# Differential attention on one core: values in halves between the heads, two output sums ahead of the last head, raw tiles of 4 KB

## The chip, the core and the metric

The kernel runs on one core of one Trainium2 chip. The metric is the device time of one execution in microseconds (us), the median of several runs. Engines are named as in the profile: PE is TensorE's matmul, PEld its weight load, DVE VectorE, ACT ScalarE, POOL GpSimd, SP SyncE, which issues the DMAs here.

## What is computed

Two layers of a transformer trunk on 512 tokens of width 1024, in float32. Each layer is a feed-forward block, a token mixer, a cross-attention into 256 memory tokens and a second feed-forward block, each followed by a layer norm. The mixer of layer 0 is differential attention; the mixer of layer 1 pools. The change lies in differential attention alone:

```python
q, k, v = jnp.split(x @ w_qkv, 3, axis=-1)       # 8 heads; q, k: 2 maps of 64; v: 128 wide
q, k = rope(q, c5, s5), rope(k, c5, s5)
...
s = jnp.where(mask, q k^T * scale, min)           # for both maps of a head
p = jax.nn.softmax(s, axis=-1)
a = p[:, :, 0] - lam * p[:, :, 1]
o = a @ v                                         # per head
...
o = o * rsqrt(mean(o * o) + eps) * subln_g * (1 - lam_init)
return o.reshape(B, S, H * 2 * dk) @ w_o
```

## The kernel before

Every float32 matmul is made of three: each factor is split into a high and a low part, and `mm3` (line 219) issues high x high, high x low and low x high into the same sums, 24 matmuls for a column block of 512 over the depth of 1024. I call one such group of three a triple. Weights come from memory into a raw tile by one DMA on SP's queue, ACT casts the raw tile to its high part (`wh`), and DVE subtracts for the low part (`wl`). The tags `wh` and `wl` have five slots each in this stage, of 4 KB per partition; `raw` has two slots of 8 KB.

**The stage of attention** is woven from two streams (`weave`, line 228). The main stream, `da_main` (line 1251), is a generator of projections: after each triple it yields the time that the planner books for it, `3 * max(107, columns * 0.42)` ns: 645 for 512 columns and 323 for 256. The side stream, `da_side` (line 1278), is one head's chain of small steps after another. It yields a weight after each step, and the next step is emitted when main has booked weight x `GAP` = 900 ns more. A step that isn't allowed yet yields `WAIT`, and the credit is set to zero. Head h may start when main's clock is `LEAD` = 6000 ns past the time at which its key was finished. When main is exhausted, what is left of the side stream is emitted without anything between (`drain`, line 242).

The emitted order is the priority by which a list scheduler fills each engine's queue with the help of its own model of times: an operation that it thinks not ready can be passed by later ones, and on the chip every queue then runs strictly in the order laid down. So the last three score matmuls of head 7 stand behind some output sums that were emitted after them.

**Main** goes over pairs of heads. `da_values` (line 1113) loads the value weights of a pair (256 columns, 1 MB, one raw tile), splits them into two tiles of `wh` and `wl`, and computes the values of all 512 tokens in two blocks of 16 triples of 256 columns, two token tiles in each block; after a block the sums are split into a value tile `v` (four slots). `raw_heads` (line 279) loads the query or key weights of a pair, 512 KB for each head, and `cols_rope` (line 287) splits those of one head. Then for each head 8 triples of 512 columns for the query, the rotation `da_rope` (line 1129: shuffle and multiply on DVE, a multiply on POOL, an add on DVE) with a split, and the same for the key. Pairs 0 to 2 have their values ahead of their heads; pair 3 (`V_FIRST` = 6) behind them. At the end of main stand eight output sums over heads 0 to 3 (`to_tokens`, line 513: four triples of 512 columns and an add on DVE for each half and token tile, rows of `da_w_o` through `rows`, line 310, four at a time). So main's order is values 0, heads 0 and 1, values 1, heads 2 and 3, values 2, heads 4, 5, 6 and 7, values 3, sums.

**Side**, for each head: `da_scores` (line 1150), 24 matmuls into six PSUM banks, then for each of four row blocks and two maps a DVE operation that adds the mask and takes the maximum (L1174) and an exponential on ACT; then `STEPS` (line 46). A mix (`da_mix`, L1190 to L1192) combines the two maps on DVE and is queued behind the last mask; turn i (`da_turn`) transposes i + 1 blocks on TensorE and splits them on ACT and DVE; last turns out the head before (`da_turn_out`: four transposes, and a split into `oT`); out i (`da_out`) is i + 1 pairs of matmuls against the values. After out 1 and out 3 the sums are copied and added, and after out 3 a root on POOL and a scaling of `o` follow. A mix yields no weight. The weights `W` (line 39): 4.6 after the scores, (1.0, 1.0, 1.2, 1.5) for the turns, (0.8, 0.8, 1.2, 2.0) for the outs, 0.8 for the last head's scaling, 1.0 for last: 15.1 for a whole head.

Behind the weave `diff_attention` (line 1303) adds the second half of the output sums, over heads 4 to 7. Of the first two of these sums five triples (heads 4 to 6) are put ahead of the last head's transposes (`ready` = 3), and they use the two PSUM banks of the tag `mm`; their weights are split into tiles of `qk`, `low` and `p` that the heads have left.

Of the kernel before, what the change touches and what calls it, by code (L numbers as in the profile page):

```python
# [17 lines left out]
P = 128  # L18
D = 1024
S = 512  # L20
NT = S // P
KC = D // P
# [4 lines left out]
ALPHA = (2 * DEPTH) ** 0.25  # L27
EPS = 1e-5
DA_H = 8
# [5 lines left out]
BAND = P + 16  # L35


V_FIRST, LEAD, GAP = 6, 6000, 900
W = dict(
    scores=4.6,  # L40
    turn=(1.0, 1.0, 1.2, 1.5),
    out=(0.8, 0.8, 1.2, 2.0),
    scale=0.8,
# [66 lines left out]
def drain(units):  # L110
    for _ in units:
        pass
# [7 lines left out]
class Trunk:  # L120
# [65 lines left out]
    @contextmanager  # L186
    def stage_pools(self, w, raw, order):

        with ExitStack() as ctx:
            self.stage = {}  # L190
            for n in order:
                if n == "wh" == order[0]:
                    self.to_w(ctx)
                if n == "mem":
                    self.to_x(ctx)
                self.stage[n] = ctx.enter_context(self.pool(n))
            self.banks = {n: ctx.enter_context(self.pool(n, space=PSUM)) for n in ("px", "py", "yz")}
            self.w_bufs, self.raw_bufs, self.aux_turn = w, raw, 0
            yield

    def raw_tile(self, shape, tag="raw"):
# [26 lines left out]
    def weave(self, main, side, gap, lead=0):  # L228


        self.clock, credit, weight = 0, -lead, 1.0
        for ns in main:
            self.clock += ns
            credit += ns
            while credit >= gap * weight:
                credit -= gap * weight
                weight = next(side, WAIT)
                if weight is WAIT:
                    credit, weight = 0, 1.0
                weight = weight or 1.0  # L240
        self.clock = float("inf")
        drain(side)
# [33 lines left out]
        self.split_weights(w[0], w[1], raw[:, :, j * P : (j + 1) * P])  # L276
        return w

    def raw_heads(self, w, c0):

        raw = self.raw_tile((2, KC, P))
        for j in range(2):
            c = c0 + j * P
            self.nc.sync.dma_start(raw[:, j], w[:, c : c + P].rearrange("(k p) n -> p k n", p=P))
        return raw

    def cols_rope(self, raw, j, wait=False):

        nc = self.nc
        w = self.hl([P, 8, P])  # L290
        src = raw[:, j].rearrange("p k (m h q e) -> p (k m) q h e", m=2, h=2, q=2)
        hi, lo = (t.rearrange("p k (m q h e) -> p (k m) q h e", m=2, q=2, h=2) for t in w)
        nc.scalar.copy(hi, src)
        with self.tc.issue_after(self.turned[1].ins) if wait else nullcontext():
            for q in range(2):
                self.last_low = nc.vector.tensor_sub(
                    lo[:, :, q], src[:, :, q], hi[:, :, q].bitcast(F32)
                )
        return w
# [10 lines left out]
    def rows(self, w, k0, kn, c0, homes=None):  # L310


        got = []
        for k in range(0, kn, 4):
            n = min(4, kn - k)
            raw = self.raw_tile((4, S))
            r0 = (k0 + k) * P
            self.nc.sync.dma_start(
                raw[:, :n], w[r0 : r0 + n * P, c0 : c0 + S].rearrange("(k p) n -> p k n", p=P)
            )  # L320
            if homes:
                got += [home() for home in homes]
                for j, t in enumerate(got):
                    self.split(t[0], t[1], raw[:, j])
                continue
            for j in range(0, n, 2):
                t = self.hl([P, 2, S])
                self.split_weights(t[0], t[1], raw[:, j : j + 2])
                got += [(t[0][:, i], t[1][:, i]) for i in range(2)]
        return got  # L330
# [182 lines left out]
    def to_tokens(self, parts, w, k0, kn, first, last, scale, homes=(None, None), ready=None):  # L513

        nc = self.nc
        ws, sums = [None, None], []
        self.sum_begins, self.sum_ends = [], []
        ready = ready or kn
        for n, (half, t) in enumerate(LAST if last else sorted(LAST)):
            c = slice(half * S, (half + 1) * S)  # L520
            if t == 0:
                ws[half] = self.rows(w, k0, kn, half * S, homes[half])

            def some(ps, t, ks):
                o = slice(t * P, (t + 1) * P)
                for k in ks:
                    h = parts[k]
                    ns = self.mm3(ps, (h[0][:, o], h[1][:, o]), ws[half][k], k == 0, k == kn - 1, ready < kn)
                    if k == 0:
                        self.sum_begins.append(self.first_mm)  # L530
                    yield ns

            if n == 0 and ready < kn:
                out_turns = self.turns
                for tok in range(2):
                    sums.append(self.mm("ps"))
                    yield from some(sums[tok], tok, range(ready - tok))
                for turn in out_turns:
                    self.queue_behind(turn, self.last_mm)
                yield from some(sums[1], 1, (ready - 1,))  # L540
            if n < len(sums):
                ps = sums[n]
                yield from some(ps, t, range(ready, kn))
            else:
                ps = self.mm("ps")
                yield from some(ps, t, range(kn))
            self.sum_ends.append(self.last_mm)
            if last:
                self.summed(half, t, scale if first else 1.0, ps)
            else:  # L550
                X = self.X[t][:, c]
                nc.vector.scalar_tensor_tensor(
                    X, X, scale if first else 1.0, ps, ALU.mult, ALU.add
                )


    def ffn(self, layer, j, ln, beside=()):
# [552 lines left out]
        nc.vector.tensor_scalar(n, n, LAM_INIT, -1.0, ALU.add, ALU.mult)  # L1110
        return n

    def da_values(self, h, vs):

        raw = self.raw_cols(self.a["da_w_qkv"][0], 2 * D + h * P)
        ws = self.wide(raw)
        for t in range(0, NT, 2):
            ps = self.mm("v").rearrange("p (t n) -> p t n", t=2)
            for i in range(2):
                o = (t + i) * P  # L1120
                for k in range(KC):
                    yield self.mm3(ps[:, i], self.xs(k, o, o + P), ws[k], k == 0, k == KC - 1)
            self.turn_late()
            v = self.act("v", (P, 2, 2, 2, P))
            ps = ps.rearrange("p t (h n) -> p t h n", h=2)
            self.split(v[:, :, :, 0], v[:, :, :, 1], ps)
            vs += [v[:, i] for i in range(2)]

    def da_rope(self, ps):
        nc = self.nc  # L1130
# [119 lines left out]

    def da_main(self):

        w, w_o = self.a["da_w_qkv"][0], self.a["da_w_o"][0]
        self.turn_late(1)
        for n in range(0, DA_H, 2):
            vs = []
            if n < V_FIRST:
                yield from self.da_values(n, vs)
            rq, rk = self.raw_heads(w, n * P), self.raw_heads(w, D + n * P)
            for h in range(n, n + 2):  # L1260
                q = self.mm("q")
                ws = self.cols_rope(rq, h % 2, h == 0)
                yield from self.project(q, ws)
                q = self.da_query(q)
                k = self.mm("k")
                ws = self.cols_rope(rk, h % 2, h == 0)
                if h == 0:
                    with self.tc.issue_after(self.last_low.ins):
                        self.nlam = self.lam()
                yield from self.project(k, ws)  # L1270
                k = self.da_key(k)
                sm = self.small("sd", (P, NT, 2))
                self.heads.append((self.clock, {"h": h, "q": q, "k": k, "v": vs, "sm": sm}))
            if not vs:
                yield from self.da_values(n, vs)
        yield from self.to_tokens(self.oT[:4], w_o, 0, 4, True, False, ALPHA)

    def da_side(self):

        for h in range(DA_H):  # L1280
            while h >= len(self.heads) or self.clock < self.heads[h][0] + LEAD:
                yield WAIT
            st = self.heads[h][1]
            self.da_scores(st, h and self.heads[h - 1][1])
            yield W["scores"]
            for step, i in STEPS:
                if step == "out":
                    while len(st["v"]) < NT:
                        yield WAIT
                if step == "last":  # L1290
                    if h:
# [383 lines left out]
        self.apart = APART["ffn"]  # L1675
        return self.stage_pools(4, dict(ra=4, rc=3), ("wh", "wl", "ra", "rc"))

    def other_pools(self, order=("wh", "wl", "raw")):
        return self.stage_pools(5, dict(raw=2), order)

    def ffn_phase(self, **more):
        bufs = dict(b1=1, b3=1, b2=1, b4=1, _x=0, xe=6, hb=4, sp=4, ha=4, sr=1, hr=3)
# [17 lines left out]
    def mixer(self, layer, ln):  # L1700
        self.apart = APART["pool" if layer else "da"]
        if layer == 0:
            bufs = dict(low=4, rt=2, a=4, p=8, o=2, qk=8, _x=0, v=4, _w=0, oT=11, mask=1)
            with self.other_pools(), self.phase_pool(("v", "v"), "rt", **bufs):
                self.diff_attention(layer, ln)
            self.close_side()
        else:
# [4 lines left out]
            bufs = dict(p=4, pw=1, gb=2, _x=0, pooled=16, sq=1)  # L1712
            with self.phase_pool(("gb", "gb"), "sq", **bufs):
# [3 lines left out]
                w = self.a["xa_wkv"][layer]  # L1717
# [52 lines left out]
```

## Time and profile before

| | us |
|---|---|
| median of 3 runs (lowest, highest) | 1911.06 (1910.82, 1911.43) |
| the profiled execution | 1912.99 |
| its span, first to last instruction | 1911.2 |
| TensorE's matmuls busy in the span | 1892.7 |
| attention stage, from the first values to the next stage's start | 338 to 590 |

The page gives busy time by engine, the chain that ended last, and groups of instructions by line. A busy PE row counts matmuls that overlap, so two questions are asked of the trace besides: who waited for whom, and in which order the instructions ran around a wait. A timeline row gives start, length (of all merged instructions), engine, line, operation, tiles and count, and in brackets the idle time before it with what ended it.

### The profile page before, as it was taken

Reading aid. Unit: us, or ns where it says so; the run is one execution under the profiler, and the core shown is the slowest. Engines: PE = TensorE matmul, PEld = TensorE weight load, DVE = VectorE, ACT = ScalarE, POOL = GpSimd, SP = SyncE. Lnnn points to the kernel's source line nnn. Section 1 sums busy time; section 2 is a strip of 40 time slices with the busy share of each in tenths; the row PEclk is TensorE's granted clock in tenths of the full one; section 3 lists DMA queues with packets and bytes.
Section 4 is the critical chain, followed back from the end, with each engine's and each line's share of the span. In section 5 each row is a group of like instructions: output and inputs, shape, how many; then the busy total and the mean of one; then the engine's idle time right before and its main releaser. Section 6 shows DMA issues by size and latency. Waiting matters only on the chain.

```text
span 1911.2 us, 32565 instructions
## 1 busy us (share of the span) xinstructions
PE 1892.7 (99%) x13136; PEld 1733.1 (91%) x13136; DVE 1550.2 (81%) x2250; ACT 1003.2 (52%) x1546; POOL 317.2 (17%) x274
## 2 busy tenths in 40 slices
PE   9999999999999999999999999999999999999998
PEld 8999998888878988999998999999899889999997
DVE  7888889888867458889888988898797568998886
ACT  6555554566645435645554655455455436555552
POOL 3112120111110002221220311212130012211210
PEclk9999999999999999999999999999999999999999
DMA  9978772323224317987785687878334438867861
GB/s 249 216 167 186 168 147 80 91 67 89 89 67 159 113 62 197 190 176 165 141 191 176 112 179 163 185 165 181 110 133 133 136 85 173 181 155 166 189 132 55
DMA packets 246743, 277.96 MB, mean 145 GB/s; under 512 B 8256, under 2 KB 212544, under 8 KB 246592
## 3 DMA queue, kind: packets, MB, share of 16 engines
q0 software_dynamic: 92928, 92.29, 31.4%
q1 hardware_dynamic: 153664, 183.59, 29.5%
q8 instruction: 103, 1.69, 0.4%
q14 instruction: 48, 0.39, 0.1%
HBM read 273.75 MB, written 2.10 MB: 144 GB/s over the span
## 4 chain that ended last, share of the span: by engine, by line
PE 86%; DVE 9%; ACT 2%; DMA 1%; issue 1%; POOL 1%; SPq 0%; DVEq 0%; ACTq 0%; POOLq 0%
PE x L223 7%; PE x L224 7%; PE x L225 7%; PE z L223 4%; PE z L224 4%; PE z L225 4%; PE ps L223 4%; PE ps L225 4%; PE ps L224 4%; PE px L223 2%; PE px L225 2%; PE px L224 2%; PE pt L509 2%; PE y L225 2%; PE x L760 2%; PE pz L225 2%
## 5 line engine op out<-in xcount | busy, mean ns | idle before, releaser
L728 POOL DMA_DIRECT2D ra<-in_ffn_w_in_dram x132 | 170.7, 1314 | 981.5 <-DVE wl L735 823.5
L733 ACT CAST wh<-ra 128x1024 fp32r<-128x1024 f32 x176 | 185.1, 1053 | 208.7 <-PE x L224 67.6
L735 DVE TENSOR_TENSOR wl<-ra,wh 128x1024 fp32r<-128x1024 f32 x176 | 214.0, 1220 | 66.1 <-ACT wh L733 65.7
L223 PE MATMUL x<-xe,wh 128*128 128x256 f32 x704 | 195.0, 277 | 0.0
L224 PE MATMUL x<-xe,wh 128*128 128x256 f32 x704 | 194.9, 277 | 0.0
L225 PE MATMUL x<-xe,wl 128*128 128x256 f32 x704 | 194.8, 277 | 0.0
L733 ACT CAST wh<-rc 128x1024 fp32r<-128x1024 f32 x132 | 139.0, 1053 | 102.3 <-PE x L224 41.6
L136 ACT CAST wh<-b 128x1024 fp32r<-128x1024 f32 x112 | 117.8, 1052 | 132.4 <-PE x L224 67.7
L735 DVE TENSOR_TENSOR wl<-rc,wh 128x1024 fp32r<-128x1024 f32 x132 | 159.9, 1218 | 24.6 <-ACT wh L733 24.5
L137 DVE TENSOR_TENSOR wl<-b,wh 128x1024 fp32r<-128x1024 f32 x112 | 136.7, 1220 | 41.0 <-ACT wh L136 41.0
L223 PE MATMUL x<-xh,wh 128*128 128x256 f32 x536 | 148.7, 278 | 0.0
L224 PE MATMUL x<-xl,wh 128*128 128x256 f32 x536 | 148.4, 277 | 0.0
L225 PE MATMUL x<-xh,wl 128*128 128x256 f32 x536 | 148.4, 277 | 0.0
L223 PEld LDWEIGHTS x<-xe,wh 128*128 128x128 f32 x704 | 132.3, 188 | 1.3
L224 PEld LDWEIGHTS x<-xe,wh 128*128 128x128 f32 x704 | 132.3, 188 | 1.4
L225 PEld LDWEIGHTS x<-xe,wl 128*128 128x128 f32 x704 | 132.2, 188 | 0.0
L137 DVE TENSOR_TENSOR wl<-raw,wh 128x1024 fp32r<-128x1024 f32 x64 | 82.3, 1294 | 40.6 <-ACT wh L136 39.9
L223 PEld LDWEIGHTS x<-xh,wh 128*128 128x128 f32 x536 | 100.8, 188 | 0.7
L224 PEld LDWEIGHTS x<-xl,wh 128*128 128x128 f32 x536 | 100.7, 188 | 0.7
L225 PEld LDWEIGHTS x<-xh,wl 128*128 128x128 f32 x536 | 100.6, 188 | 0.0
L136 ACT CAST wh<-raw 128x1024 fp32r<-128x1024 f32 x64 | 66.4, 1050 | 60.2 <-PE xq L224 18.5
L223 PE MATMUL z<-xe,wh 128*128 128x256 f32 x352 | 97.5, 277 | 0.0
(447 smaller groups left out, 6261.2 us busy)
## 6 DMA issues: line engine op xcount, KB each, us to landing
ra<-in_ffn_w_in_dram POOLq DMA_DIRECT2D x132, 512.0 KB, 6.9
rc<-in_ffn_w_in_dram SPq DMA_DIRECT2D x88, 512.0 KB, 5.5
b<-in_ffn_w_out_dram SPq DMA_DIRECT2D x76, 512.0 KB, 4.7
ra<-in_ffn_w_in_dram SPq DMA_DIRECT2D x44, 512.0 KB, 4.8
rc<-in_ffn_w_in_dram POOLq DMA_DIRECT2D x44, 512.0 KB, 7.7
raw<-in_xa_wkv_dram SPq DMA_DIRECT2D x16, 1024.0 KB, 5.4
raw<-in_da_w_qkv_dram SPq DMA_DIRECT2D x16, 512.0 KB, 5.0
raw<-in_xa_wq_dram SPq DMA_DIRECT2D x8, 1024.0 KB, 5.3
```

Of the source, the lines that this page charges most:

```text
L136: self.nc.scalar.copy(hi, src),
L137: self.nc.vector.tensor_sub(lo, src, hi.bitcast(F32)),
L223: self.first_mm = mm(out, w[0], x[0], start=start, stop=False, skip_group_check=again)
L224: mm(out, w[0], x[1], start=False, stop=False, skip_group_check=again)
L225: self.last_mm = mm(out, w[1], x[0], start=False, stop=stop, skip_group_check=again)
L509: self.turns = [self.nc.tensor.transpose(pt[:, j], b, self.ident) for j, b in enumerate(blocks)]
L728: nc.gpsimd.dma_start(t, source(*block), accum_op=ALU.add)
L733: hi = nc.scalar.copy(v[0], raw)
L735: lo = nc.vector.tensor_sub(v[1], raw, v[0].bitcast(F32))
L760: self.last_mm = nc.tensor.matmul(ps[:, j], v[i][:, k, j * P : (j + 1) * P], x[l][:, k], start=n == i == l == 0, stop=n == 7 and i == 1, s ...
```

## The change

Main becomes a list of steps, `MAIN`. The values of a pair are made in two halves (a half is one block of two token tiles), and one half stands between every two heads, a pair ahead of its use. Two of the eight output sums stand ahead of head 7, six behind it. The weight after the scores goes from 4.6 to 5.8; all other weights, `LEAD` and `GAP` stay. The raw tiles of this stage are four of 4 KB instead of two of 8 KB: value weights, and the rows of the output weights, come in two DMAs of 512 KB instead of one of 1 MB, query and key weights in one of 512 KB for each head as before, but asked for head by head. The step out waits for the value tiles up to its own block, not for all four.

```diff
-V_FIRST, LEAD, GAP = 6, 6000, 900
+LEAD, GAP = 6000, 900
+MAIN = (
+    ("v", (0, 0)), ("v", (0, 2)), ("qk", 0), ("v", (1, 0)), ("qk", 1), ("v", (1, 2)),
+    ("qk", 2), ("v", (2, 0)), ("qk", 3), ("v", (2, 2)),
+    ("qk", 4), ("v", (3, 0)), ("qk", 5), ("v", (3, 2)), ("qk", 6),
+    ("sums", 2), ("qk", 7), ("sums", 6),
+)
 W = dict(
-    scores=4.6,
+    scores=5.8,
...
+            self.raw_rows = 2 if raw == dict(raw=4) else 4
...
         for ns in main:
+            ns = ns or 0
...
-    def cols_rope(self, raw, j, wait=False):
+    def cols_rope(self, c0, wait=False):
...
+        raw = self.raw_block(self.a["da_w_qkv"][0][:, c0 : c0 + P].rearrange("(k p) n -> p k n", p=P))
...
-        for k in range(0, kn, 4):
-            n = min(4, kn - k)
-            raw = self.raw_tile((4, S))
+        for k in range(0, kn, self.raw_rows):
+            n = min(self.raw_rows, kn - k)
+            raw = self.raw_tile((self.raw_rows, S))
...
             if homes:
-                got += [home() for home in homes]
-                for j, t in enumerate(got):
+                for j in range(n):
+                    t = homes[k + j]()
                     self.split(t[0], t[1], raw[:, j])
+                    got.append(t)
...
                     X, X, scale if first else 1.0, ps, ALU.mult, ALU.add
                 )
+                yield None
...
+    def raw_block(self, src):
+
+        raw = self.raw_tile((4, 256))
+        home = raw.rearrange("p a b -> p (a b)").rearrange("p (k n) -> p k n", k=src.shape[1])
+        self.nc.sync.dma_start(home, src)
+        return raw
+
+    def da_value_weights(self, h):
+
+        c = 2 * D + h * P
+        w = self.a["da_w_qkv"][0][:, c : c + 256].rearrange("(k p) n -> p k n", p=P)
+        ws = []
+        for j in range(0, KC, 4):
+            t = self.hl([P, 4, 256])
+            self.split_weights(t[0], t[1], self.raw_block(w[:, j : j + 4]))
+            ws += [(t[0][:, i], t[1][:, i]) for i in range(4)]
+        return ws
+
+    def da_values(self, ws, t, vs):
...
+        vs, ws = {}, {}
+        sums = self.to_tokens(self.oT, w_o, 0, 4, True, False, ALPHA)
+        for step, n in MAIN:
+            if step == "sums":
+                for _ in range(n):
+                    yield from iter(lambda: next(sums), None)
+                continue
+            if step == "v":
+                pair, half = n
+                if half == 0:
+                    vs.setdefault(pair, [])
+                    ws[pair] = self.da_value_weights(2 * pair)
+                yield from self.da_values(ws[pair], half, vs[pair])
+                continue
+            q = self.mm("q")
+            yield from self.project(q, self.cols_rope(n * P, n == 0))
...
-                    while len(st["v"]) < NT:
+                    while len(st["v"]) <= i:
                         yield WAIT
...
-            with self.other_pools(), self.phase_pool(("v", "v"), "rt", **bufs):
+            with self.other_pools(raw=4), self.phase_pool(("v", "v"), "rt", **bufs):
```

More of the change, by code (lines that the diff above doesn't have):

```diff
@@ L277, in cols @@
         return w
[L279 to L285, printed above, removed]
-    def cols_rope(self, raw, j, wait=False):
+    def cols_rope(self, c0, wait=False):
         nc = self.nc
         w = self.hl([P, 8, P])
-        src = raw[:, j].rearrange("p k (m h q e) -> p (k m) q h e", m=2, h=2, q=2)
+        raw = self.raw_block(self.a["da_w_qkv"][0][:, c0 : c0 + P].rearrange("(k p) n -> p k n", p=P))
+        src = raw.rearrange("p a b -> p (a b)").rearrange("p (c h q e) -> p c q h e", h=2, q=2, e=16)
         hi, lo = (t.rearrange("p k (m q h e) -> p (k m) q h e", m=2, q=2, h=2) for t in w)
@@ L1111, in lam @@
         return n
[L1113 to L1127, printed above, removed]
+    def raw_block(self, src):
[13 more added lines that the diff above has]
+    def da_values(self, ws, t, vs):
+        ps = self.mm("v").rearrange("p (t n) -> p t n", t=2)
+        for i in range(2):
+            o = (t + i) * P
+            for k in range(KC):
+                yield self.mm3(ps[:, i], self.xs(k, o, o + P), ws[k], k == 0, k == KC - 1)
+        self.turn_late()
+        v = self.act("v", (P, 2, 2, 2, P))
+        ps = ps.rearrange("p t (h n) -> p t h n", h=2)
+        self.split(v[:, :, :, 0], v[:, :, :, 1], ps)
+        vs += [v[:, i] for i in range(2)]
     def da_rope(self, ps):
@@ L1251, in da_main @@
     def da_main(self):
-        w, w_o = self.a["da_w_qkv"][0], self.a["da_w_o"][0]
+        w_o = self.a["da_w_o"][0]
         self.turn_late(1)
[L1255 to L1276, printed above, removed]
+        vs, ws = {}, {}
[14 more added lines that the diff above has]
+            yield from self.project(q, self.cols_rope(n * P, n == 0))
+            q = self.da_query(q)
+            k = self.mm("k")
+            wk = self.cols_rope(D + n * P, n == 0)
+            if n == 0:
+                with self.tc.issue_after(self.last_low.ins):
+                    self.nlam = self.lam()
+            yield from self.project(k, wk)
+            k = self.da_key(k)
+            v = vs.setdefault(n // 2, [])
+            sm = self.small("sd", (P, NT, 2))
+            self.heads.append((self.clock, {"h": n, "q": q, "k": k, "v": v, "sm": sm}))
     def da_side(self):
@@ L1676, in ffn_pools, with other_pools @@
         return self.stage_pools(4, dict(ra=4, rc=3), ("wh", "wl", "ra", "rc"))
-    def other_pools(self, order=("wh", "wl", "raw")):
-        return self.stage_pools(5, dict(raw=2), order)
+    def other_pools(self, order=("wh", "wl", "raw"), raw=2):
+        return self.stage_pools(5, dict(raw=raw), order)
     def ffn_phase(self, **more):
```

## The prediction

> **What bounds the kernel now.** I read the page first, then busy time by stretch, then TensorE's waits, and last the order of time around each of them.
>
> ```profile
> span 1911.2 us, 32565 instructions
> PE 1892.7 (99%) x13136; PEld 1733.1 (91%) x13136; DVE 1550.2 (81%) x2250; ACT 1003.2 (52%) x1546; POOL 317.2 (17%) x274
> ```
>
> TensorE (PE) is busy for 99% of the span, so the change can win only what TensorE loses in the one stage that it touches. It adds or removes no matmul, transpose, split, mask or exponential; it moves them. The attention stage runs from 338 us (first values) to 590 us:
>
> ```profile
> 338.00:590.00 252.00, 246.22 (x1564) 211.15 (x1563) 201.84 (x485) 142.00 (x372) 41.83 (x55) 1.00 0.29 88
> 438.00:463.00 25.00, 25.00 (x147) 20.75 (x145) 22.44 (x58) 15.42 (x43) 5.87 (x8) 1.00 0.27 80
> 463.00:485.00 22.00, 20.79 (x125) 16.86 (x122) 19.77 (x51) 13.78 (x40) 4.37 (x7) 1.00 0.24 71
> 485.00:507.00 22.00, 20.66 (x133) 17.40 (x131) 19.67 (x52) 13.28 (x36) 4.92 (x6) 1.00 0.26 93
> ```
>
> The columns behind the length are busy us of PE, weight loads, DVE, ACT and POOL, then granted clock, DMA share and GB/s. TensorE is idle 5.78 us of the 252. DVE comes next with 80%, and 90% in the stretches where heads 3 to 5 run. The waits of the same window, all that the view lists:
>
> ```profile
> PE pt L509 <- DVE p L1192: 4.4, 5, 1.3
> PE ps L223 <- DVE X L375: 0.6, 1, 0.6
> PE pk L224 <- DVE mem4l L137: 0.5, 1, 0.5
> ```
>
> Five waits of 4.4 us are one mechanism: the first transposes of a head's probabilities (the step turn) come before DVE has mixed its two maps (L1192). The other two lie behind the woven part and stay. In order of time, for heads 4 and 5 (the two longest):
>
> ```profile
> 468.37 0.39 PE L224 MATMUL k<-xl,wh 128*128 128x512 f32 x1
> 468.60 0.40 PE L225 MATMUL k<-xh,wl 128*128 128x512 f32 x1
> 470.20 0.33 PE L509 MATMUL pt<-ident,p 128*128 128x128 f32 x1 [1.21 <-DVE p L1192]
> 493.35 0.33 PE L509 MATMUL pt<-ident,p 128*128 128x128 f32 x1 [1.34 <-DVE p L1192]
> ```
>
> Matmuls overlap: the next starts 0.23 us after the last (468.37, 468.60), though each lasts 0.40. A wait therefore costs its idle time and 0.17 us of lost overlap: 4.4 + 5 x 0.17 = 5.2 us in all. That is the pot.
>
> The Trainium skill (Perfetto Trace Analysis, Identifying the Most-Contended Engine) calls matmul busy time a bad measure and takes that of weight loads. By it the stage would have 252 - 211 = 41 us of room. The rows above speak against that here: a 512-wide matmul every 0.23 us covers a shorter weight load, and that is no gap which an order can close. The 5.2 us stand.
>
> **Why DVE is late.** Head 4, its first scores matmul on TensorE, then DVE:
>
> ```profile
> 462.48 0.33 PE L1165 MATMUL sc<-qk 64*128 64x128 f32 x2
> 464.59 0.50 PE L223 MATMUL k<-xh,wh 128*128 128x512 f32 x1
> 464.67 0.68 DVE L296 TENSOR_TENSOR wl<-raw,wh 128x512 fp32r<-128x512 f32 x1
> 465.45 0.69 DVE L142 SCALAR_TENSOR_TENSOR qk<-rt,qk 128x512 fp32r<-128x512 f32 x1
> 466.06 0.28 DVE L1174 CUSTOM_DVE_ANT_0 p<-sc,mask 128x128 f32<-128x128 f32 x1
> 468.73 0.69 DVE L1174 CUSTOM_DVE_ANT_0 p<-sc,mask 128x512 f32<-128x512 f32 x1
> 469.80 0.74 DVE L1192 SCALAR_TENSOR_TENSOR p<-p,cf 128x128 f32<-128x128 f32 x2
> ```
>
> The scores start at 462.48 and take TensorE 2.1 us (the next key matmul starts at 464.59), but the first mask only at 466.06, 3.6 us later, behind the rotation of a query whose projection has just ended and behind a weight split. From first to last mask's end it is 3.36 us (466.06 to 469.42). Where the scores follow values instead, as for head 1:
>
> ```profile
> 390.56 0.33 PE L1165 MATMUL sc<-qk 64*128 64x128 f32 x2
> 392.62 0.28 DVE L1174 CUSTOM_DVE_ANT_0 p<-sc,mask 128x128 f32<-128x128 f32 x1
> 396.37 0.74 DVE L1192 SCALAR_TENSOR_TENSOR p<-p,cf 128x128 f32<-128x128 f32 x2
> ```
>
> Here the mask comes 2.1 us after the scores, the mix 5.8 us after them, and TensorE does not wait.
>
> **The change, part by part.** *The weight of the scores, 4.6 to 5.8.* The planner books a 512-wide triple of matmuls at 645 ns and emits the next side step once weight x 900 ns are booked: 4140 ns (six triples) stood between scores and first transposes, now 5220 ns, eight with what credit is left over. Two triples are 2 x 3 x 0.23 = 1.4 us more cover. Head 4 lacked 1.21 + 0.17 = 1.38 us, head 5 1.51; the shorter three lacked less. So even with DVE as late as now, some 0.1 us is left: -5.1 us.
>
> *Values one half between every two heads.* A head's turn becomes 16 triples of query and key (10.3 us booked) and 16 of 256 columns (5.2): 15.5 against a side chain of 16.3 x 0.9 = 14.7, the same for heads 1 to 5. Scores may start 6.0 us after the head is pushed, and side steps are taken after whole triples, hence 1.3 to 1.9 us behind the values: head 1's case in all heads, not head 4's. This is a second cover for the same 5.2 us and can't be counted twice. Query weights, key weights and a pair's two value tiles share five slots; two are now held across two projections, which leaves three, and a projection's weights still have the 10.3 us before it free. I take 0. The step out now asks only for the value blocks that it reads, and the values are a pair ahead, so that wait never holds; the yields of None and the homes taken row by row move no instruction: 0.
>
> *Two sums ahead of head 7.* This and the longer chain move the end. By the planner's sums main ends at 144.5 us in both. Before, head 7's scores come at 131.6 and its last output step (out 3) 13.1 x 0.9 = 11.8 later, 143.4: a triple before the end. Now keys of head 7 are done at 129.0, scores come at 136.1, and out 3 would need 12.9 more, 149.0. So out 1, turn 3, out 2 and out 3 fall behind the end of main, where only five triples of the next sums (heads 4 to 6) are there as filler. The end of head 7 before:
>
> ```profile
> 545.42 0.60 PE L509 MATMUL pt<-ident,p 128*128 128x128 f32 x4
> 545.78 0.48 PE L223 MATMUL ps<-wh,oT 128*128 128x512 f32 x1
> 546.68 0.69 DVE L137 TENSOR_TENSOR a<-pt,a 128x512 fp32r<-128x512 f32 x1 [0.97 <-ACT a L136]
> 549.33 0.28 PE L1213 MATMUL po<-v,a 128*128 128x256 f32 x1
> 550.21 0.45 PE L223 MATMUL ps<-wh,oT 128*128 128x512 f32 x1
> 550.41 0.37 ACT L1219 COPY o<-po 128x256 f32<-128x256 f32 x1 [2.27 <-PE po L1214]
> 552.52 1.04 POOL L1233 TENSOR_TENSOR f<-f,mhalf 128x4 f32<-128x4 f32 x1
> 553.60 0.70 ACT L1242 ACTIVATE o<-o,f 128x128 f32<-128x128 f32 x2 [1.49 <-POOL f L1233]
> 554.38 0.60 PE L509 MATMUL pt<-ident,o 128*128 128x128 f32 x4
> ```
>
> Turn 3 takes 0.36 us (545.42 to 545.78), its halves are ready at 547.37, 1.95 after its start; out 3 takes 0.88 (549.33 to 550.21); copy, root on POOL and scaling until the last transposes take 4.17 (550.21 to 554.38), and six triples of 0.69 filled them without a hole. Scaled by blocks, turn 2 is 0.27, out 1 0.44, out 2 0.66. In the new order, from turn 2 on: turn 2 and out 1 0.71, then turn 3 to its halves 1.95, out 3 0.88, chain 4.17: 7.7 us. TensorE's work in it: 0.27 + 0.44 + 0.36 + 0.66 + 0.88 + five triples 3.4 = 6.0. Hole: 1.7 us, new. Its bounds: 0, if steps of head 7 slip ahead of main's last triples, and 1.7 + 1.4 = 3.1, if the late output halves (two operations like L142's 0.69) stand before turn 3's on DVE. I take 1.7, since nothing else can fill it: the next sums have but two PSUM banks.
>
> *Raw tiles of 4 KB.* Four slots for two; loads of 1 MB of values and of output weights become two of 512 KB, seven more SP issues in this stage.
>
> ```profile
> raw<-in_da_w_qkv_dram SPq DMA_DIRECT2D x16, 512.0 KB, 5.0
> raw<-in_xa_wkv_dram SPq DMA_DIRECT2D x16, 1024.0 KB, 5.4
> ACT wh L136 <- DMA raw<-in_da_w_qkv_dram: 3.5, 1, 3.5
> ```
>
> A load of half the size lands hardly sooner (5.0 for 5.4 us), but four can fly. Only one cast in the stage waited for values' weights, and TensorE not at all; SP has only loads queued behind. 0, with 3.5 us as the upper bound for one that reaches TensorE. The Trainium skill (DMA: Bandwidth & Descriptors, Measured) says to batch loads to 1 MiB and more; the two landing times agree with it, and by it this part loses. With the stage's DMA share at 0.29 I give it a small chance.
>
> *Sum:* -5.1 + 0 + 1.7 + 0 = -3.4 us. The profiled run took 1912.99 us for its span of 1911.2, 1.9 above the median of 1911.06; I put the difference on the median: 1907.7 us.
>
> **The rivals.** *The end costs nothing.* If the list scheduler lets head 7's steps pass main's last triples, only the pot counts: 1911.06 - 5.2 = 1905.9. For it: six triples fitted 4.17 us exactly. Against: a step's priority is its place of emission.
>
> *The query's rotation gets in front of the mix (slower).* Head 5 shows it:
>
> ```profile
> 484.58 0.44 PE L1165 MATMUL sc<-qk 64*128 64x128 f32 x4
> 489.39 0.75 DVE L1132 STREAM_SHUFFLE rt<-k 128x512 f32<-128x512 f32 x1
> 492.08 0.69 DVE L1135 TENSOR_TENSOR rt<-rt 128x512 f32<-128x512 f32 x1 [1.24 <-POOL rt L1134]
> 492.95 0.74 DVE L1192 SCALAR_TENSOR_TENSOR p<-p,cf 128x128 f32<-128x128 f32 x2
> ```
>
> The projection had ended with the scores, its shuffle and sum went ahead of the mix, and DVE stood for POOL, strictly in order; the transpose came 8.8 us after the scores (484.58 to 493.35). In the new order every head's next query ends five or six triples behind its scores, 2.1 + 5 x 0.69 = 5.5 us after their start, and is emitted ahead of the mix; the last mask ends 2.1 + 3.4 = 5.5 us after it by head 1. It decides which is first. If the rotation wins in heads 0 to 6, the transposes, due at 2.1 + 8 x 0.69 = 7.6, wait 1.2 us each: 8.4 - 5.2 + 1.7 = +4.9, 1916.0. Against: mask and mix need no POOL, and in head 1 the mix follows the masks at once.
>
> *The waits stay.* The Trainium skill (Perfetto Trace Analysis, Optimization Strategy) says that the same gap again and again can mean too few buffers. Were the mix late for a buffer of p (eight, one head's), new cover would be eaten by a later start, and only the end's price would be left: 1911.06 + 1.7 = 1912.8. Against: DVE works without a pause from 464.67 to the mix.
>
> *Half-size loads come late:* one wait of 3.5 us reaches TensorE, 1911.2.
>
> **How the numbers follow.** A measurement of this kernel can tell 0.2%, 3.8 us, from no change, so the bounds are 1907.2 and 1914.9. Forecast 0.60 (1907.7; own range 1906.3 to 1909.4, two fifths of it past the bound: 0.24 faster, 0.36 same), end free 0.17 (faster), rotation first 0.12 (slower), waits stay 0.08 and late loads 0.03 (same). Faster 0.41, same 0.47, slower 0.12. The range leaves out the rotation: from 1905.4 (the free end less 0.5, about the spread of the three runs, 1910.82 to 1911.43) to 1913.0 (waits that stay).
>
> **What would show it.** Right: waits of transposes for L1192 in the woven part fall from 4.4 us to under 0.5; the first mask comes about 2 us after the scores in heads 1 to 5; a new wait of 1 to 2 us before the last transposes of o, with out 1 to out 3 of head 7 back to back. Wrong: waits for L1192 in heads 0 to 6 with L1135 ahead of the mix; casts that wait for raw; or no hole at the end.

## The result and the profile after

The changed kernel takes 1908.39 us (median of 21 runs, 1906.26 to 1911.29), the kernel before 1912.29 (21 runs, 1910.82 to 1916.15). The ratio is 0.9978 with a 95% interval of 0.9972 to 0.9985: faster by 0.22%, some 4.2 us, between 2.9 and 5.4. By the two medians it is 3.9 us. Two slow executions, one of lead9 (1946.03 us) and one of last_light (3839.91 us), are left out of the ratios below, and nothing is read from last_light's profile, which was of the latter.

The page of the changed kernel, its first two lines:

```profile
span 1909.5 us, 32582 instructions
PE 1894.1 (99%) x13136; PEld 1734.0 (91%) x13136; DVE 1549.4 (81%) x2250; ACT 1004.3 (53%) x1546; POOL 318.1 (17%) x274
```

The number of instructions of each compute engine is as before. The span is only 1.7 us shorter: this execution came to the stage 1.3 us later, with as many matmuls and DVE instructions up to there, and took 0.6 us more behind it. So I measure the stage by itself, from the first matmul of the values to the first key matmul of the cross-attention. (The window of 338 to 590 us in the first table and in the prediction reaches past that matmul, which starts at 578.69.) The two ends before, then after, from the order of time:

```profile
338.76 0.36 PE L223 MATMUL v<-wh,xh 128*128 128x256 f32 x1
578.69 0.39 PE L223 MATMUL pk<-mem4h,wh 128*128 128x256 f32 x1
```

```profile
340.10 0.36 PE L230 MATMUL v<-wh,xh 128*128 128x256 f32 x1
576.38 0.38 PE L230 MATMUL pk<-mem4h,wh 128*128 128x256 f32 x1 [0.44 <-ACT mem4h L142]
```

239.93 us have become 236.28: 3.65 less. A second execution of the changed kernel gave 236.44, so in these two the stage repeats within 0.2 us, where the 21 runs of the whole kernel spread over five. TensorE's waits in the stage, all that the view of the changed kernel lists between 338 and 590 us (L511 is the transposes' line now, L1210 the mix, L1260 the scaling):

```profile
PE pt L511 <- ACT o L1260: 0.7, 1, 0.7
PE ps L230 <- DVE X L377: 0.6, 1, 0.6
PE pk L231 <- DVE mem4l L143: 0.5, 1, 0.5
PE pk L230 <- ACT mem4h L142: 0.4, 1, 0.4
```

The five waits for the mix, 4.4 us, are gone. In their place there is one of 0.7 us at the end of head 7. The last line is new to the list too: the first key matmul of the cross-attention, with which the stage ends, waits 0.4 us for the split of the memory tokens. Head 4 in order of time, as it stands in the prediction for the kernel before (scores, first mask, mix, first transposes; TensorE's rows, then DVE's):

```profile
462.26 0.33 PE L1183 MATMUL sc<-qk 64*128 64x128 f32 x2
469.98 0.27 PE L511 MATMUL pt<-ident,p 128*128 128x128 f32 x1
```

```profile
463.77 0.29 DVE L1192 CUSTOM_DVE_ANT_0 p<-sc,mask 128x128 f32<-128x128 f32 x1 [2.16 <-PE sc L1183]
467.53 0.74 DVE L1210 SCALAR_TENSOR_TENSOR p<-p,cf 128x128 f32<-128x128 f32 x2
```

DVE now waits for the scores, not the scores for DVE: the first mask comes 1.5 us after them (3.6 before), the mix 5.3 (7.3 before), and the transposes 7.7 us after them, without a wait. Heads 0 to 6 all look like this: first mask at 1.5 to 2.2 us, mix at 5.3 to 5.9, transposes at 7.7 or 7.8.

The end of the stage after the change, from head 7's turn 2 to its last transposes:

```profile
544.18 0.49 PE L511 MATMUL pt<-ident,p 128*128 128x128 f32 x3
...
545.50 0.40 PE L230 MATMUL ps<-qk,oT 128*128 128x512 f32 x1
545.74 0.40 PE L231 MATMUL ps<-qk,oT 128*128 128x512 f32 x1
546.20 0.33 PE L1232 MATMUL po<-v,a 128*128 128x128 f32 x1
...
546.82 0.33 PE L1231 MATMUL po<-v,a 128*128 128x256 f32 x1
547.25 0.33 PE L1232 MATMUL po<-v,a 128*128 128x128 f32 x1
...
550.91 0.39 PE L232 MATMUL ps<-qk,oT 128*128 128x512 f32 x1
551.96 0.44 PE L511 MATMUL pt<-ident,o 128*128 128x128 f32 x2 [0.66 <-ACT o L1260]
```

A hole shows as a start that comes later than its kind does elsewhere: 551.96 - 550.91 is 1.05 where 0.23 is usual, 0.82 lost; 546.20 - 545.74 loses 0.23 in the same way, and 547.25 - 546.82 loses 0.26 against the 0.17 that is usual between the two matmuls of a pair when another pair runs just ahead. In all 1.31 us.

### The profile page after: what moved, and what is told of

Its sections match the earlier page's. It is cut to its first block, busy times and chain, and to the rows that moved or that the text cites. A ratio compares the mean times of both kernels' runs of the same rounds, so it can differ in the third digit from the quotient of the medians.

```text
span 1909.5 us, 32582 instructions
## 1 busy us (share of the span) xinstructions
PE 1894.1 (99%) x13136; PEld 1734.0 (91%) x13136; DVE 1549.4 (81%) x2250; ACT 1004.3 (53%) x1546; POOL 318.1 (17%) x274
## 4 chain that ended last, share of the span: by engine, by line
PE 85%; DVE 9%; DMA 2%; ACT 2%; issue 1%; POOL 1%; SPq 0%; DVEq 0%; ACTq 0%; POOLq 0%
PE x L230 7%; PE x L231 7%; PE x L232 7%; PE z L230 4%; PE z L231 4%; PE z L232 4%; PE ps L230 4%; PE ps L232 4%; PE ps L231 4%; PE px L230 2%; PE px L232 2%; PE px L231 2%; PE y L232 2%; PE x L763 2%; PE y L230 2%; PE y L231 2%
```

## The experiments

The theory: both the place of the scores (behind values instead of behind a projection) and the heavier weight take the five waits away, each nearly alone; the end then loses the chain behind head 7's out 3 to too little filler. Rivals: only one of the two does it; the sums ahead of head 7 or the raw slots are what counts; the hole at the end can't be closed.

| kernel | stage, us | ratio to the kernel before, 95% interval |
|---|---|---|
| before | 239.93 | |
| changed | 236.28 | 0.9978 [0.9972, 0.9985] |
| changed, again | 236.44 | 0.9982 [0.9974, 0.9991] |
| order_w46 | 236.86 | 0.9983 [0.9974, 0.9991] |
| weight_only | 237.51 | 0.9985 [0.9976, 0.9994] |
| sums8 | 239.63 | 1.0000 [0.9991, 1.0009] |
| sums1 | 237.02 | 0.9985 [0.9976, 0.9994] |
| raw2 | 236.44 | 0.9982 [0.9973, 0.9991] |
| lead9 | 246.39 | 1.0031 [1.0022, 1.0040] |
| last_light2 | 234.90 | 0.9973 [0.9962, 0.9984] |
| light_lead5 | 237.93 | 0.9989 [0.9980, 0.9998] |

The intervals are about 0.1% wide on either side, near 2 us, so the times tell only the large differences apart; the small ones are read from the stage and its waits.

**order_w46**: the new order with the old weight.

```diff
-    scores=5.8,
+    scores=4.6,
```

> The changed kernel with the weight after the scores back at 4.6; order, sums and raw tiles as changed. Theory (order): values between the heads bring the first mask to 1.5 to 2.2 us behind the scores, so the mix starts 5.3 to 5.9 us behind them, and a transpose due at 2.1 + 6 x 0.69 = 6.2 us finds it ready or lacks at most 0.2 us: waits for L1192's successor under 0.5 us in sum, and the end has one step less behind main, a hole of about 1 us where the changed kernel has 1.4. Stage length (first values matmul to first key matmul of the cross-attention; 239.9 before, 236.3 changed) 236.0, time 1908. Rival (weight): the weight alone is the cover, so the waits of 4.4 us return and the stage is 240.

The order alone brings 3.1 of the 3.65 us. Two waits for mixes are left, by start to start 0.28 us at head 1 and 0.51 at head 6, where the first mask came 2.5 and 2.9 us after the scores. The wait at the end is the same 0.7, but of the two small holes ahead of it one of 0.2 is left, so the hole is 1.0 us, as forecast. The theory holds, its 236.0 was too low by 0.9.

**weight_only**: the kernel before with the new weight.

```diff
-    scores=4.6,
+    scores=5.8,
```

> The kernel before with the weight 5.8 instead of 4.6, nothing else. Theory (order and weight are two covers for the same wait): two triples more cover take away 1.4 us of each of the five waits, 4.4 us falls to under 0.4; head 5 keeps 0.1 or more since the rotation stands ahead of its mix. The last head's out 3 falls behind main, so the end gets a hole of 0.7 us (chain 4.17 against five triples 3.4). Stage 235.6 to 236.5, time 1908 to 1909, as good as the whole change. Rival (order): with the old order DVE is late by more when the side chain is longer, and 2 us or more of the waits remain: stage 238 or more.

The waits for the mix fall from 4.4 us to 0.07, though the first masks come no earlier on the whole (2.5 to 3.4 us after the scores in heads 0 to 5, where it was 1.5 to 3.6). But another step takes their place. Its line in the list of waits, and DVE's rows where it first comes:

```profile
PE po L1214 <- DVE a L137: 1.2, 2, 0.9
```

```profile
378.49 0.68 DVE L1135 TENSOR_TENSOR rt<-rt 128x512 f32<-128x512 f32 x1
379.09 0.28 DVE L137 TENSOR_TENSOR a<-pt,a 128x128 fp32r<-128x128 f32 x1
```

The low half of the first probabilities stands behind the key's rotation (L1135), and TensorE's out 0 waits 0.91 us for it. So the weight alone brings 2.4 us: between the two theories, and 1 us short of the least that I expected.

**sums8**: no output sum ahead of head 7.

```diff
-    ("sums", 2), ("qk", 7), ("sums", 6),
+    ("qk", 7), ("sums", 8),
```

> The changed kernel with all eight output sums behind head 7 (weights and order else as changed). By the planner head 7's scores come at 134.8 of its clock, not 136.1, and one step more fits ahead of main's end. Theory (the end's hole is what the two sums cost): the hole of 1.4 us shrinks by 0.3 to 0.6, no new wait, stage 235.8, time 1908. Rival (the two sums are needed as filler for head 6): head 6 runs beside head 7's projections anyway, so if it is right, new waits for mixes or halves of 0.5 us or more appear between 505 and 530 us, and the stage is 236.8 or longer.

The rival wins, and by more than it claimed: nearly the whole gain is gone, in the stage and in the times. Head 6 in the order of time, TensorE's rows and then DVE's:

```profile
506.31 1.71 PE L1183 MATMUL sc<-qk 64*128 64x128 f32 x19
508.52 0.96 PE L1183 MATMUL sc<-qk 64*128 64x512 f32 x5 [0.50 <-ACT po L1241]
516.02 0.33 PE L511 MATMUL pt<-ident,p 128*128 128x128 f32 x1 [0.82 <-DVE p L1210]
...
518.66 0.50 PE L230 MATMUL ps<-wh,oT 128*128 128x512 f32 x1 [0.70 <-DVE rt L1151]
```

```profile
507.35 0.67 DVE L1151 TENSOR_TENSOR rt<-q,ropeC 128x512 f32<-128x512 f32 x1
511.26 0.69 DVE L148 SCALAR_TENSOR_TENSOR qk<-rt,qk 128x512 fp32r<-128x512 f32 x1 [0.70 <-ACT qk L147]
511.87 0.29 DVE L1192 CUSTOM_DVE_ANT_0 p<-sc,mask 128x128 f32<-128x128 f32 x1
```

Without the sums, nothing stands between head 6's key and head 7's query, as nothing did between the two heads of a pair in the kernel before: the query's rotation is on DVE when the scores come, the first mask follows 5.6 us after them, and the weight of 5.8 doesn't cover that. The late mix is one loss of three: the last scores wait for a copy on ACT (L1241), and the output sums for the rotation of head 7's key (L1151). Start to start the three are 0.9, 1.0 and 0.9 us of the 3.35. The two sums do for head 6 what a half of values does for the others. And the hole at the end was for the most part not theirs: the wait for the scaling is 0.7 us here too, and with the small hole of 0.2 ahead of it it comes to 1.0.

**sums1**: one sum ahead.

```diff
-    ("sums", 2), ("qk", 7), ("sums", 6),
+    ("sums", 1), ("qk", 7), ("sums", 7),
```

> The changed kernel with one output sum ahead of head 7 and seven behind it. By the planner head 7's query then ends two triples after head 6's scores start, as in the kernel before at head 5. Theory (what counts is where the scores fall in the next head's projections): the rotation of that query gets in front of head 6's mix, its first transposes come 8.4 to 8.9 us after its scores and wait 0.7 to 1.2 us; head 7's end gains at most 0.3; stage 236.9 to 237.4, between the changed kernel's 236.3 and 239.6 with no sum ahead. Rival (the sums are filler by their amount): half of the loss with none ahead, stage 238, and no rotation in front of the mix.

As the theory has it. DVE at head 6, whose scores start at 504.55:

```profile
509.37 0.74 DVE L1150 STREAM_SHUFFLE rt<-q 128x512 f32<-128x512 f32 x1
...
512.05 0.69 DVE L1153 TENSOR_TENSOR rt<-rt 128x512 f32<-128x512 f32 x1 [1.24 <-POOL rt L1152]
...
512.92 0.74 DVE L1210 SCALAR_TENSOR_TENSOR p<-p,cf 128x128 f32<-128x128 f32 x2
```

The masks come early (1.5 us after the scores), yet the rotation stands ahead of the mix and DVE waits 1.24 us for POOL, as at head 5 of the kernel before. The first transposes come 8.8 us after the scores (513.32) and lose 0.79 us start to start. Half the sums, a fifth of the loss (0.7 of 3.35 us): it goes by place, not by amount.

**lead9**: the rotation ahead of the mix in heads 0 to 6, by starting their scores later.

```diff
-LEAD, GAP = 6000, 900
+LEAD, GAP = 9000, 900
```

> The changed kernel with LEAD 9000 instead of 6000, so that the scores of heads 0 to 6 start one or two triples before the next query's end. It puts the slower rival of the prediction to the test in every head. That rival: the rotation stands ahead of the mix, the first transposes come 8.8 us after the scores where they were due at 7.7, so seven waits of 1.1 us, 7.7 in all; head 7's later start adds 1 to 2 at the end; stage 245, time 1917. Theory (mixes are pushed by priority of emission only where the rotation is ready before the last mask): the same. Against both: the weight of 5.8 covers any phase, waits under 2 us in sum, stage under 239.

This is the prediction's slower rival, made to happen: 8.77 us from scores to transposes in heads 0 to 5, 8.87 in head 6, and the waits:

```profile
PE pt L511 <- DVE p L1210: 6.2, 7, 0.9
PE pt L511 <- ACT o L1260: 1.5, 1, 1.5
```

Each of the seven costs 1.05 us start to start (7.3 in all), and the end loses 1.7 instead of 0.8, since all of head 7's steps from the last-step on stand behind main. Most of the rest of the 10.1 us by which the stage is longer than the changed kernel's comes right behind that wait, where the clock falls too (last section). The kernel is slower than before.

**raw2**: two raw slots of 8 KB.

```diff
-            with self.other_pools(raw=4), self.phase_pool(("v", "v"), "rt", **bufs):
+            with self.other_pools(raw=2), self.phase_pool(("v", "v"), "rt", **bufs):
```

> The changed kernel with two raw slots of 8 KB as before; loads of values and of query and key weights still 512 KB each, output weights again 1 MB. So at most two loads of the projections are under way where four were. Theory (loads have slack): casts wait for raw tiles more often, TensorE not at all; stage 236.3 within 0.3, time 1908.4. Rival (four slots are what makes the new order work): a projection's weights come late, TensorE waits for wl or wh in the stage by 1 us or more, stage 237.3 or longer.

ACT's casts wait for loads of the projections' weights, which they nowhere do by the changed kernel's list:

```profile
ACT wh L294 <- DMA raw<-in_da_w_qkv_dram: 5.5, 3, 3.0
ACT wh L142 <- DMA raw<-in_da_w_qkv_dram: 2.2, 2, 1.7
```

7.7 us of ACT's idle time, and none of it reaches TensorE: the stage is 236.44, as in the second execution of the changed kernel. Four slots are no part of the gain. The new order with value loads of 1 MB was not run; that the smaller loads cost nothing rests on TensorE waiting for no load in either kernel.

**last_light** and **last_light2**: lighter weights for head 7 alone. With f = 0.6 for h = 7 and 1.0 for the others:

```diff
-            yield W["scores"]
+            f = 0.6 if h == DA_H - 1 else 1.0
+            yield f * W["scores"]
...
-                        yield W["last"]
+                        yield f * W["last"]
...
-                    yield W[step][i]
+                    yield f * W[step][i]
```

> The changed kernel with head 7's weights (all but the last scaling) times 0.6, so that by the planner its out 3 falls one triple before main's end again. Theory (the end's hole is the chain behind out 3 against too little filler): the wait of the last transposes for the scaling (0.7 us) and the two small holes in front of it go, 1.4 us in all; nothing new by more than 0.3, since the scores still have 5 triples behind them and its mix starts 6.3 us after them. Stage 235.0, time 1907. Rival (the lighter steps only move the hole: halves are late for head 7's outs instead): stage 236.0 or more with new waits of po for halves of 0.5 us or more.

> The kernel with head 7's weights times 0.6 once more, since the first profile of it was of an execution at twice the time. Theory (the end's hole is the chain behind out 3 against too little filler): the wait for the scaling (0.7 us) and the small holes ahead of it go; stage 234.8 to 235.2, ratio 0.997. Rival (the hole only moves): new waits of head 7's outs or transposes of 0.5 us or more, stage 236.

last_light's times gave 0.9969 [0.9957, 0.9981]. The waits of last_light2 in the stage:

```profile
PE ps L230 <- DVE X L377: 0.6, 1, 0.6
PE pk L231 <- DVE mem4l L143: 0.5, 1, 0.5
PE pk L230 <- ACT mem4h L142: 0.4, 1, 0.4
```

The wait for the scaling is gone, and so are the two small holes ahead of it: 234.90, 1.38 less than the changed kernel, for a hole of 1.31. The hole was the chain against its filler, and it can be closed by the order alone. This version beats both kernels by the stage; by the times it is below the changed one (0.9969 and 0.9973 for 0.9978), but the intervals overlap.

**light_lead5**: the same, with head starts 1 us earlier.

```diff
-LEAD, GAP = 6000, 900
+LEAD, GAP = 5000, 900
```

> Head 7's weights times 0.6 and LEAD 5000, a version that may beat the changed kernel: out 3 of head 7 stands four triples ahead of main's end, so the chain behind it has nine triples (6.2 us) for its 4.2 and the wait for the scaling is gone; the first masks now meet the split of the values and come up to 0.7 us later, still covered by the weight of 5.8. If all of it holds: stage 234.8 to 235.2, as last_light2, since a wait that is gone can't go twice. If head 0's or head 6's scores meet the key's rotation instead, a wait of up to 1 us comes back and the stage is 236.

That was wrong by 3 us. The scores of heads 1 and 3 now start right at the end of the values or one triple later, and new waits come:

```profile
PE po L1232 <- DVE a L143: 1.2, 2, 0.8
PE sc L1183 <- ACT po L1241: 0.7, 1, 0.7
```

Their first masks come 3.2 us after the scores, behind the split of the values and two splits of weights, and the chain meets other DVE work later on, as in weight_only. Not the mixes but the halves and the banks of the scores are late.

**after_again**: the changed kernel once more.

> The changed kernel as it is, to see how far a stage length and a set of runs repeat. Stage 236.3 within 0.3, waits as in its profile (0.7 us for the scaling, none for mixes), ratio 0.998.

236.44 us, the same four waits of the same lengths, ratio 0.9982: the two executions differ by 0.16 us in the stage.

## Why the prediction was right, and where not

*The pot.* 4.4 us of idle time in five waits and 0.17 us of overlap for each, 5.2 us: all of it was won (5.1 us, start to start). Nothing waits for a mix any more. Of the 41 us of room that the share of weight loads would leave, the best version here reaches 5.0 (239.93 - 234.90).

*The two covers.* Right that weight and order cover the same wait and can't be added: 2.4 and 3.1 us alone, 3.65 together. But the prediction's sum puts -5.1 us on the weight, even with DVE as late as before, and neither cover is worth that alone: the weight pushes the next steps into the rotation (1.2 us for halves), and the order without the weight leaves two mixes 0.3 and 0.5 us late.

*The end.* The chain from turn 2 was forecast at 7.7 us and took 7.78 (544.18 to 551.96); the hole was forecast at 1.7 and is 1.3. The filler is the five triples of the forecast (15 matmuls), two of whose matmuls ran between the outs; TensorE's work in the chain took 7.78 - 1.31 = 6.5 us, not 6.0, so less of it was idle. The mechanism and nearly the size are right, and last_light2 shows the cause.

*Two sums ahead of head 7.* Here a step failed. I booked them, with the longer chain, only as what moves the end: a cost. They cost 0.3 us there (the hole is 1.3 us with them and 1.0 without), and without them the stage is 3.35 us longer: they are the piece between head 6 and head 7's query. I had counted head 6 among the heads whose scores follow values ("head 1's case in all heads"), and did not ask what stands in the values' place.

*Raw tiles.* 0, as forecast. That a load of half the size lands hardly sooner did not hold: the rows of the output weights took 4.9 us from issue to landing in loads of 1 MB and 3.3 in loads of 512 KB. The rule of the Trainium skill (DMA: Bandwidth & Descriptors, Measured; there for loads issued from GpSimd) to batch loads to 1 MiB did not bear on the time here, with loads of 512 KB and TensorE not waiting for one.

*The rivals.* The rotation ahead of the mix is real, with nearly the price given (8.8 us; 1.05 for 1.2 us each in lead9), and the point from which it decides is nearly the one named, whether the projection ends before the last mask. Where the rotation went ahead of the mix (head 5 before, head 6 in sums1, heads 0 to 6 in lead9), the projection had ended 0.9 to 1.8 us before the last mask's end; in heads 0, 2 and 4 of the kernel before it had ended 0.1 to 0.4 us before it, and the rotation still came behind the mix. In the changed kernel it ends 0.9 to 1.7 us after it. That the waits stay for lack of buffers is refuted: no buffer of p was added. Late loads did not come: TensorE waits for none in the changed kernel, nor in raw2, where the casts do. The end free of cost did not happen by itself.

*The sum.* -3.4 us forecast; 3.65 in the stage, 4.2 (2.9 to 5.4) in the times. Of its terms 5.1 was won and 1.3 lost at the end; another 0.3, start to start, is lost at the cross-attention's first key matmul, for which the prediction had no term, and why that wait grew was not looked into. Time and range hold: 1908.39 in 1905.4 to 1913.0. The kernel before took 1912.29 in these runs, 1.2 us more than the 1911.06 from which the forecast starts, so the difference is the better test of it. That it came out on the "faster" side of 0.2%, which had 0.41, and not in "same" with 0.47, is less than the runs can tell: the interval of the ratio spans the bound.

## What to carry to other kernels

Where one engine is full and another runs in strict order beside it, look at what the second has in its queue when a step's input arrives; moving the step by one projection can be worth more than a heavier gap, and a gap that covers one wait moves the next step into another. Put a piece of independent work (values, or early output sums) between one head's key and the next head's query everywhere, ahead of the last head too, and lighten the weights of the last chain so that it ends before its filler does. Measure such changes by the stage in the trace: two executions agreed within 0.2 us where the whole kernel spreads over five.

## What the hardware showed besides

In lead9 TensorE's granted clock fell at the end of the stage. Busy us and clock by stretch (after the length: PE, weight loads, DVE, ACT, POOL, then the clock):

```profile
556.00:558.00 2.00, 0.72 (x4) 0.25 (x2) 0.22 (x2) 0.51 (x3) 1.24 (x2) 1.00 0.71 193
558.00:560.00 2.00, 1.22 (x7) 0.84 (x7) 0.38 (x3) 1.16 (x3) 0.00 (x0) 0.98 0.92 294
560.00:562.00 2.00, 2.00 (x5) 1.61 (x6) 0.64 (x1) 0.00 (x0) 0.00 (x0) 0.50 1.07 374
562.00:564.00 2.00, 1.64 (x5) 0.83 (x5) 1.30 (x4) 0.00 (x0) 0.00 (x0) 0.66 0.95 314
```

Two gaps, of 1.52 and 0.54 us, left TensorE busy 1.94 of 4 us; the clock was then 0.50 for 3.4 us (559.93 to 563.35), and 512-wide matmuls started 0.42 to 0.43 us apart (560.50, 560.92, 561.35) instead of 0.23, about 1 us lost over five of them. The changed kernel's gap of 0.66 us at the same place left the clock at 1.00. The Trainium skill (TensorE: Matmul & The Clock Gate, Why this matters for your kernels) asks for no idle gap above some 3 us between bursts; here the clock fell after two gaps close together, the longer about half of that, and the measurement decides. But it is one case, and what the clock goes by is not shown: in sums8 a gap of 1.65 us far ahead of the stage, with TensorE busy little more, left it at 1.00.

```profile
22.50:26.50 4.00, 2.18 (x17) 1.90 (x16) 1.77 (x3) 3.04 (x4) 0.00 (x0) 1.00 1.13 304
```
